# FFN 1's second matmul with seven tile pairs, four of them partly made ahead, in a streaming-encoder layer

## The chip, the cores and the metric

The kernel runs on one core of a Trainium2 chip, in one launch. The metric is the device time of a run in microseconds (us). The engines have short names in the profile: PE (TensorE, the matmuls), PEld (its weight loads, beside the matmuls), DVE (VectorE), ACT (ScalarE), POOL (GpSimd) and SP (SyncE, which here issues transfers only). SBUF is the memory on the chip beside the engines, PSUM holds the sums of matmuls in 8 banks of 128 x 512 fp32, and weights come from DRAM by transfers (DMA).

## The reference

One encoder layer on 512 tokens of width 1024, all in fp32. Two feed-forward layers (FFN) of inner width 2816 stand around a mixer of a recurrent branch and a windowed attention:

```python
def rms_norm(x, g):
    y = x * lax.rsqrt(jnp.mean(x * x, axis=-1, keepdims=True) + 1e-6)
    return y * g

def swiglu(x, w1, w3, w2):
    return (jax.nn.silu(x @ w1) * (x @ w3)) @ w2

f = swiglu(rms_norm(h, pre_g1), w1, w3, w2)          # FFN 1
h = h + 0.5 * rms_norm(f, post_g1)
u = rms_norm(h, mix_pre_g)
...                                                   # mixer: projections of u, scan, attention, gates
h = h + rms_norm(merged @ w_o, mix_post_g)
f = swiglu(rms_norm(h, pre_g2), w1, w3, w2)          # FFN 2
h = h + 0.5 * rms_norm(f, post_g2)
```

## The kernel before

**Precision.** Every operand of a matmul is split into a high part (a ScalarE copy to the float32r type) and a low part (a VectorE subtraction), and each product is three matmuls: high by high, high by low, low by high. `split2`, `split_to` and `task` with `flush` do the splits.

**The first matmuls of an FFN.** w1 and w3 have 22 column tiles each, named w1a, w3a for FFN 1 and w1b, w3b for FFN 2. FFN 1 computes the first `NC1` = 6 tiles of each in the plain way. The other 16 go in twos through `Pairs.run`: a job takes two neighbouring tiles of w1 or of w3 as a 2 x 2 matrix of blocks (a11, a12 are the halves of the first tile, a21, a22 of the second) and computes with seven block products instead of eight. There are 16 jobs, w1 and w3 in turn, numbered from 0; FFN 2 has 20. For a job VectorE forms four weight sums (`prep(m, 0)`): s12 = [a21 + a22 | that - a11] and s34 = [a11 - a21 | a12 - that]; steps 1 to 4 of `prep` split the tiles and the sums. In `run`, three PSUM banks bu, bx, bc take the products; ScalarE copies partial results to the tile ct (q1, q5, u), and VectorE adds them to later products: the result c = [c11 | c12; c21 | c22] of 256-token blocks. w1's result goes through SiLU, w3's is multiplied into it. The eighth block step of a job, `last`, runs inside the next job. A job prepares steps 1 to 4 of the next job and step 0 of the one after, and asks for the raw tiles of the job after that (`raws(n + 3)`). So a job has seven products of 12 matmuls of 256 columns; the first job has six.

**The order of work.** `point()` is called after each product of a job (and after each 12 matmuls of a plain unit, a half unit). `later(n, fn, rank)` puts work at the n-th point from now, lower rank first. The engines run their own queues in this order and wait for each other through the tiles only, so SyncE may issue a load as soon as the SBUF slot for it is free, long before the others come to the same place. There are `NSLOT` = 43 slots of 4 KB a partition; raw tiles, split tiles, sums and hidden tiles all use them.

**The second matmul.** `w2_gemm` multiplies the 22 hidden tiles by w2. `W2[name]` gives (W2_A, sizes, RF, fill): W2_A plain tiles first, then groups of tile pairs, the last RF tiles in `tok_finish` with the norms. A pair again takes seven products in place of eight; its weights are b11 and b21 (`w_b1`, one split of the first raw tile), t1 and t2 (`w_t12`), b22, t3 and t4. The hidden parts come from `h_plain`, `h_sums`, `h_rest`. A list of costs and due times (`plan`) is packed backwards from the due times, at 95% of VectorE's time, to find the point at which each part is made. For w2a (FFN 1) it is (6, (5,), 6, 0.95): six plain tiles, one group of five pairs, six tiles at the end. For w2b (FFN 2) it is (2, (4, 4), 4, 0.95).

**Pairs made ahead.** For the pairs in `PRE` the parts t1, t2, b22, t3 and t4 are made earlier (`pre_pair`), stored to DRAM by SyncE and loaded again in w2 (`w_load`). `PRE_AT` says in which stage, from which point and in which steps. One pair of w2a is made in the jobs of FFN 1; four pairs of w2b in the mixer's stages xr, xg and wg, five in all.

**Norms.** `post_norm` and `norms` sum squares on ScalarE, take a root (`root`), and `factor` forms a reciprocal on VectorE and one refinement step: r, e, r2. `softplus` is a chain of small VectorE steps on 8 columns, spread over the jobs.

## Time and profile before

| | |
|---|---|
| median of 3 runs | 1118.52 us (1118.45 to 1119.05) |
| the profiled execution's own time | 1118.27 us |
| its span, first to last instruction | 1116.5 us |
| granted TensorE clock, mean | 0.999 |
| busy: PE, PEld, DVE, ACT, POOL | 1107.2, 988.6, 920.1, 617.2, 34.7 us |
| transfers | 166.91 MB, mean 149 GB/s |

The pair jobs of FFN 1 run from about 78 to 234 us of the span, w2a from there to about 360, the mixer's projections from 364 on, FFN 2's jobs and w2b at the end.

A row of the groups has the line, engine and operation, out<-in by the program's names, the shapes, the count, then the busy time in us and the mean ns of one, and then the engine's idle time before these instructions with what ended it. A row of the timeline has start and duration in us. SPq and POOLq are the queues from which transfers are issued. The chain that ended last is followed back from the last instruction, at each step to what released it. Matmuls are pipelined: a PE row's duration is longer than the step from one matmul to the next.

### The profile page before, as it was taken

The page shows a single profiled execution, that of the slowest core. Times are in us where ns is not written, and L with a number is a line of the kernel's source. Part 1 is how long each engine was busy: PE and PEld are TensorE (multiplying, and loading weights), DVE is VectorE, ACT ScalarE, POOL GpSimd, SP SyncE. Part 2 cuts the span into 40 slices and gives each one's busy share as a digit, 9 for nine tenths or more (in the row PEclk, how much of TensorE's full clock was granted, in tenths as well). Part 3 has the DMA queues.
Part 4 walks back from the last instruction along what each step waited for, and adds up shares of the span by engine and source line. Part 5 has one row for each costly group of instructions (what it writes and reads, how often), then busy time and mean ns, then how long its engine had stood idle before and what let it go on. Part 6 is the DMA issues. An engine that isn't in the chain of part 4 may idle for free.

```text
span 1116.5 us, 17407 instructions
## 1 busy us (share of the span) xinstructions
PE 1107.2 (99%) x6679; PEld 988.6 (89%) x6679; DVE 920.1 (82%) x1622; ACT 617.2 (55%) x1088; POOL 34.7 (3%) x60
## 2 busy tenths in 40 slices
PE   9999999999999999999999999999999999999997
PEld 7889999988889887888888888888999999998886
DVE  5998889987987878897799876877788888887995
ACT  7455555574465468945656564456554555555352
POOL 0000000000000000001021111000000000000000
PEclk9999999999999999999999999999999999999999
DMA  9863334371565465445232235352423323257543
GB/s 353 138 163 104 114 114 131 125 274 38 170 226 182 159 226 189 153 149 200 103 95 76 84 106 196 127 186 104 161 83 107 114 85 105 95 191 283 177 179 114
DMA packets 52452, 166.91 MB, mean 149 GB/s; under 512 B 5712, under 2 KB 7248, under 8 KB 52368
## 3 DMA queue, kind: packets, MB, share of 16 engines
q1 hardware_dynamic: 49632, 156.97, 40.7%
q0 software_dynamic: 2448, 8.43, 4.0%
q8 instruction: 52, 0.85, 0.3%
q10 hardware_dynamic: 288, 0.39, 0.1%
q14 instruction: 32, 0.26, 0.1%
HBM read 139.57 MB, written 25.16 MB: 148 GB/s over the span
## 4 chain that ended last, share of the span: by engine, by line
PE 94%; ACT 3%; DVE 2%; issue 1%; DMA 0%; DVEq 0%; SPq 0%; ACTq 0%
PE c L899 11%; PE c L901 11%; PE c L900 11%; PE f L205 10%; PE f L206 10%; PE f L207 10%; PE acc L223 4%; PE acc L225 4%; PE acc L224 4%; PE acc L774 4%; PE acc L773 4%; PE acc L775 4%; PE pt L1508 1%; ACT ig_e L1308 1%; PE s L1472 1%; PE s L1471 1%
## 5 line engine op out<-in xcount | busy, mean ns | idle before, releaser
L205 PE MATMUL f<-uT,whi 128*128 128x512 f32 (+1 forms) x504 | 184.3, 366 | 0.0
L207 PE MATMUL f<-uT,whi 128*128 128x512 f32 (+1 forms) x504 | 182.7, 362 | 0.0
L206 PE MATMUL f<-uT,wlo 128*128 128x512 f32 (+1 forms) x504 | 182.7, 362 | 0.0
L899 PE MATMUL c<-Xh,whi 128*128 128x256 f32 x432 | 122.4, 283 | 0.1
L899 PE MATMUL c<-uT,whi 128*128 128x256 f32 x432 | 122.4, 283 | 0.0
L901 PE MATMUL c<-Xl,whi 128*128 128x256 f32 x432 | 122.3, 283 | 0.0
L900 PE MATMUL c<-Xh,wlo 128*128 128x256 f32 x432 | 122.3, 283 | 0.0
L901 PE MATMUL c<-uT,whi 128*128 128x256 f32 x432 | 122.3, 283 | 0.0
L900 PE MATMUL c<-uT,wlo 128*128 128x256 f32 x432 | 122.3, 283 | 0.0
L205 PEld LDWEIGHTS f<-uT,whi 128*128 128x128 f32 x504 | 95.1, 189 | 15.7 <-issue 1.3
L207 PEld LDWEIGHTS f<-uT,whi 128*128 128x128 f32 x504 | 95.1, 189 | 15.0
L206 PEld LDWEIGHTS f<-uT,wlo 128*128 128x128 f32 x504 | 95.2, 189 | 14.2
L196 DVE TENSOR_TENSOR wlo<-S,whi 128x1024 fp32r<-128x1024 f32 x72 | 87.8, 1219 | 14.2 <-ACT whi L195 14.2
L899 PEld LDWEIGHTS c<-Xh,whi 128*128 128x128 f32 x432 | 83.0, 192 | 0.3 <-ACT ct L978 0.3
L900 PEld LDWEIGHTS c<-Xh,wlo 128*128 128x128 f32 x432 | 83.0, 192 | 0.0
L899 PEld LDWEIGHTS c<-uT,whi 128*128 128x128 f32 x432 | 83.0, 192 | 0.0
L901 PEld LDWEIGHTS c<-Xl,whi 128*128 128x128 f32 x432 | 83.0, 192 | 0.0
L900 PEld LDWEIGHTS c<-uT,wlo 128*128 128x128 f32 x432 | 83.0, 192 | 0.0
L901 PEld LDWEIGHTS c<-uT,whi 128*128 128x128 f32 x432 | 83.0, 192 | 0.0
L195 ACT ACTIVATE whi<-S 128x1024 fp32r<-128x1024 f32 x72 | 72.6, 1050 | 0.0
L223 PE MATMUL acc<-whi,hT 128*128 128x512 f32 x144 | 56.2, 390 | 0.0
L224 PE MATMUL acc<-wlo,hT 128*128 128x512 f32 x144 | 56.1, 389 | 0.0
(411 smaller groups left out, 2781.7 us busy)
## 6 DMA issues: line engine op xcount, KB each, us to landing
raw_w1b<-in_w1b_dram SPq DMA_DIRECT2D x22, 512.0 KB, 4.2
raw_w3b<-in_w3b_dram SPq DMA_DIRECT2D x22, 512.0 KB, 4.3
raw_w3a<-in_w3a_dram SPq DMA_DIRECT2D x21, 512.0 KB, 4.5
raw_w2a<-in_w2a_dram SPq DMA_DIRECT2D x21, 512.0 KB, 5.7
raw_w1a<-in_w1a_dram SPq DMA_DIRECT2D x20, 512.0 KB, 4.9
raw_w2b<-in_w2b_dram SPq DMA_DIRECT2D x17, 512.0 KB, 4.3
h<-h SPq DMA_DIRECT2D x16, 512.0 KB, 3.4
raw_wg<-in_wg_dram SPq DMA_DIRECT2D x16, 512.0 KB, 4.2
```

The source lines that it names most:

```text
L195: act.activation(hi, src, AF.Copy)
L196: dve.tensor_tensor(out=lo, in0=src, in1=f32(hi), op=ALU.subtract)
L205: pe.matmul(ps[:, c0:c1], wh[:, s], h_, start=k == 0, stop=False)
L206: pe.matmul(ps[:, c0:c1], wl[:, s], h_, start=False, stop=False)
L207: pe.matmul(ps[:, c0:c1], wh[:, s], l_, start=False, stop=k == KT - 1)
L223: pe.matmul(acc[n], x[:, 0, c], wh[:, s], start=first, stop=False, skip_group_check=True)
L224: pe.matmul(acc[n], x[:, 0, c], wl[:, s], start=False, stop=False, skip_group_check=True)
L225: pe.matmul(acc[n], x[:, 1, c], wh[:, s], start=False, stop=last, skip_group_check=True)
L773: pe.matmul(b, h[:, c], wh, start=start and n_ == 0, stop=False, skip_group_check=True)
L899: pe.matmul(ps, wh[:, s], xh, start=first, stop=False, skip_group_check=True)
L900: pe.matmul(ps, wl[:, s], xh, start=False, stop=False, skip_group_check=True)
L901: pe.matmul(ps, wh[:, s], xl, start=False, stop=k == 3, skip_group_check=True)
```

## The change

FFN 1's w2 takes two plain tiles, groups of three and four pairs, and six tiles at the end. Four pairs (2, 4, 6, 8) are partly made ahead in the pair jobs, and for the same four the split of the first raw tile is made in the last jobs (`early_b1`). From job 3 on, FFN 1's jobs form two of the four weight sums in other ways: a21 is loaded from DRAM a second time into the sum's tile, and GpSimd issues a transfer that adds a22 from DRAM to it; a scaled ScalarE copy writes -a21, and another such transfer adds a11. In the jobs of both FFNs from the fourth on, the copy of the first product goes to the bank bc, and the product a12 is added to it there, so that VectorE's add falls away; SiLU and product then read the bank. `root` uses the reciprocal root in place of root and reciprocal. The tail of the last job (the first two hidden and weight tiles of w2) is divided over two places. The steps of softplus stand three points apart, and the w2b pairs in the stage xr take one step a point.

```diff
     def root(ss, v0):
-        act.activation(s, ss[:, 1:2], AF.Sqrt, scale=1.0 / D, bias=v0)
+        act.activation(s, ss[:, 1:2], AF.Abs_reciprocal_sqrt, scale=1.0 / D, bias=v0)
     def factor(ss, v0, s):
-        dve.reciprocal(r, s)
-        dve.scalar_tensor_tensor(out=e, in0=r, scalar=v, in1=r, op0=ALU.mult, op1=ALU.mult)
-        dve.scalar_tensor_tensor(out=r2, in0=e, scalar=-3.0, in1=r, op0=ALU.add, op1=ALU.mult)
+        dve.scalar_tensor_tensor(out=e, in0=s, scalar=v, in1=s, op0=ALU.mult, op1=ALU.mult)
+        dve.scalar_tensor_tensor(out=r2, in0=e, scalar=-3.0, in1=s, op0=ALU.add, op1=ALU.mult)
...
+    def early_b1(nm, f, at_):
+        k = order.index((nm, f))
+        def split():
+            hi, lo = slot([P, D], F32R, name="bh"), slot([P, D], F32R, name="bl")
+            split2(hi, lo, raws.pop(k))
+            EARLY_B1[nm, f] = hi, lo
+        later(at_ - 9, lambda: dma_one(k), 4)
+        later(at_, split, 4)
...
         def w_b1(f):
+            if (nm, f) in EARLY_B1:
+                hi, lo = EARLY_B1.pop((nm, f))
+                W[f] = {"b11": (hi[:, :QH], lo[:, :QH]), "b21": (hi[:, QH:], lo[:, QH:])}
+                return []
...
+        def plus(self, o, m, j, c):
+            pool.dma_start(out=o, in_=self.block(m, j, c), accum_op=ALU.add)
+        def sum1(self, m):
+            if self.add_from <= m < len(self.jobs):
+                self.s[m] = slot([P, 2 * QH], name="S12"), slot([P, 2 * QH], name="S34")
+                o = self.s[m][0][:, :QH]
+                sp.dma_start(out=o, in_=self.block(m, 1, 0))
+                self.plus(o, m, 1, 1)
+        def sums_ahead(self, m):
+            self.sum1(m)
+            later(SUM3, lambda: self.sum3(m), 2)
+        def sum3(self, m):
+            if self.add_from <= m < len(self.jobs):
+                o = (self.s.get(m) or self.w[m]["s"])[1][:, :QH]
+                r = raws[self.k0 + 2 * m + 1] if m in self.s else self.w[m]["r"][1]
+                act.activation(o, r[:, :QH], AF.Copy, scale=-1.0)
+                self.plus(o, m, 0, 0)
...
             if i == 0:
-                dve.tensor_tensor(out=s12[:, :QH], in0=a21, in1=a22, op=ALU.add)
+                if not self.made:
+                    dve.tensor_tensor(out=s12[:, :QH], in0=a21, in1=a22, op=ALU.add)
...
-                dve.tensor_tensor(out=s34[:, :QH], in0=a11, in1=a21, op=ALU.subtract)
+                if not self.made:
+                    dve.tensor_tensor(out=s34[:, :QH], in0=a11, in1=a21, op=ALU.subtract)
...
+                seed = n >= 3
+                h0 = 256 if seed else 0
...
                 mm_s(W["a11"], X["b11"], bu)
-                act.activation(q1, bu, AF.Copy)
+                act.activation(bc if seed else q1, bu, AF.Copy)
                 if n == len(self.jobs) - 1:
-                    tail()
+                    tail(1)
...
                 at(3)
+                if n == len(self.jobs) - 1:
+                    tail(2)
...
                 def c11():
-                    mm_s(W["a12"], X["b21"], bc)
+                    mm_s(W["a12"], X["b21"], bc, seed)
-                    dve.tensor_tensor(out=c[:, 0, :256], in0=bc, in1=q1, op=ALU.add)
+                    if not seed:
+                        dve.tensor_tensor(out=c[:, 0, :256], in0=bc, in1=q1, op=ALU.add)
+                    elif first:
+                        act.activation(c[:, 0, :256], bc, AF.Silu)
+                    else:
+                        c1 = self.c1[f]
+                        dve.tensor_tensor(out=c1[:, 0, :256], in0=bc, in1=c1[:, 0, :256], op=ALU.mult)
...
-                    act.activation(c[:, 0, :], c[:, 0, :], AF.Silu)
+                    act.activation(c[:, 0, h0:], c[:, 0, h0:], AF.Silu)
...
-                    dve.tensor_tensor(out=c1[:, 0, :], in0=c1[:, 0, :], in1=c[:, 0, :], op=ALU.mult)
+                    dve.tensor_tensor(out=c1[:, 0, h0:], in0=c1[:, 0, h0:], in1=c[:, 0, h0:], op=ALU.mult)
...
                 self.raws(n + 3)
+                self.sums_ahead(n + 3)
...
-    pairs_a = Pairs("w1a", "w3a", NC1, X1, hid)
+    pairs_a = Pairs("w1a", "w3a", NC1, X1, hid, ADD_FROM)
...
-            later(at1 + i, step, 4)
+            later(at1 + i * SP_STEP, step, 4)
...
+ADD_FROM = 3
+SUM3 = 6
-W2 = {"w2a": (6, (5,), 6, 0.95), "w2b": (2, (4, 4), 4, 0.95)}
+W2 = {"w2a": (2, (3, 4), 6, 0.95), "w2b": (2, (4, 4), 4, 0.95)}
-PRE = {"w2a": (6,), "w2b": (2, 4, 6, 8, 14)}
+PRE = {"w2a": (2, 4, 6, 8), "w2b": (2, 4, 6, 8, 14)}
-PRE_AT = {"w1a": [("w2a", 6, 63, PRE_JOB)], "xr": [("w2b", 2, 1, 2), ("w2b", 8, 6, 2), ("w2b", 14, 11, 2)], ...}
+PRE_AT = {"w1a": [("w2a", 2, 0, (0, 1, 2, 9, 10, 14, 15, 16, 17, 18, 22, 23, 29, 30, 31)), ("w2a", 4, 28, (...)), ("w2a", 6, 49, (...)), ("w2a", 8, 77, (...))], "xr": [("w2b", 2, 1, 1), ("w2b", 8, 6, 1), ("w2b", 14, 12, 1)], ...}
+EARLY = {"w1a": [("w2a", 2, 79), ("w2a", 4, 86), ("w2a", 6, 100), ("w2a", 8, 108)]}
+SP_STEP = 3
```

More of the change, by code (lines that the diff above doesn't have):

```diff
@@ L263, in root @@
         s = small(1, "s")
-        act.activation(s, ss[:, 1:2], AF.Sqrt, scale=1.0 / D, bias=v0)
+        act.activation(s, ss[:, 1:2], AF.Abs_reciprocal_sqrt, scale=1.0 / D, bias=v0)
         return s
     def factor(ss, v0, s):
-        v, r, e, r2 = (small(1, x) for x in ("v", "r", "e", "r2"))
+        v, e, r2 = (small(1, x) for x in ("v", "e", "r2"))
         dve.scalar_tensor_tensor(out=v, in0=ss[:, 1:2], scalar=1.0 / D, in1=v0, op0=ALU.mult, op1=ALU.add)
-        dve.reciprocal(r, s)
-        dve.scalar_tensor_tensor(out=e, in0=r, scalar=v, in1=r, op0=ALU.mult, op1=ALU.mult)
-        dve.scalar_tensor_tensor(out=r2, in0=e, scalar=-3.0, in1=r, op0=ALU.add, op1=ALU.mult)
+        dve.scalar_tensor_tensor(out=e, in0=s, scalar=v, in1=s, op0=ALU.mult, op1=ALU.mult)
+        dve.scalar_tensor_tensor(out=r2, in0=e, scalar=-3.0, in1=s, op0=ALU.add, op1=ALU.mult)
         return r2
@@ L535, in pre_pair @@
             later(at0 + (i * step if isinstance(step, int) else step[i]), lambda fns=fns: [fn() for fn in fns], 4)
+    EARLY_B1 = {}
+    def early_b1(nm, f, at_):
[6 more added lines that the diff above has]
+        later(at_, split, 4)
     def pre_at(where):
+        for nm, f, at_ in EARLY.get(where, ()):
+            early_b1(nm, f, at_)
         for i, at_ in FIRST_AT.get(where, ()):
@@ L685, in w2_gemm @@
                 d = 0.68 * i
-                plan += [(ta + d, 1.1, h_plain, f), (ta + d, 1.22, w_b1, f)]
+                plan += [(ta + d, 1.1, h_plain, f), (ta + d, 0 if (nm, f) in EARLY_B1 else 1.22, w_b1, f)]
                 plan += [(ta + 2 * PB + d, 2.1, h_sums, f), (ta + 4 * PB + d, 0.7, h_rest, f)]
@@ L904, in hybrid_layer, with __init__ @@
     class Pairs:
-        def __init__(self, na, nb, f0, X, hid):
+        def __init__(self, na, nb, f0, X, hid, add_from=99):
+            self.add_from = add_from
             self.jobs = [(nm, f) for f in range(f0, FT, 2) for nm in (na, nb)]
@@ L911, in __init__, with block @@
             self.k0 = order.index((na, f0))
-            self.w, self.c1 = {}, {}
+            self.w, self.c1, self.s = {}, {}, {}
+        def block(self, m, j, c):
+            nm, f = self.jobs[m]
+            return a[nm][(f + j) * P : (f + j + 1) * P, c * QH : c * QH + QH]
+        def plus(self, o, m, j, c):
[15 more added lines that the diff above has]
+                self.plus(o, m, 0, 0)
         def raws(self, m):
@@ L928, in prep @@
                     self.raws(m)
-                s12, s34 = slot([P, 2 * QH], name="S12"), slot([P, 2 * QH], name="S34")
+                self.made = m in self.s
+                s12, s34 = self.s.pop(m, None) or (slot([P, 2 * QH], name="S12"), slot([P, 2 * QH], name="S34"))
                 self.w[m] = {"r": (raws.pop(k), raws.pop(k + 1)), "s": (s12, s34)}
@@ L1244, in hybrid_layer, with w2_ahead @@
     }
-    def w2_ahead():
-        hid.to(1)
-        split_to(st["split"] + 1)
-        hid.to(2)
+    def w2_ahead(n):
+        hid.to(n)
         split_to(st["split"] + 1)
     pre_at("w1a")
-    softplus(6, 9)
+    softplus(*SP_AT)
     pairs_a.run(w2_ahead, late)
```

3 lines of the change are left out of this document (2 added, 1 removed).

## The prediction

> **What bounds the kernel now.** I read the page's busy times first, then the shares of the chain that ended last, then that chain in order of time, the windows by stage, the groups by line, and last the transfer queue's own rows.
>
> ```profile
> span 1116.5 us, 17407 instructions
> PE 1107.2 (99%) x6679; PEld 988.6 (89%) x6679; DVE 920.1 (82%) x1622; ACT 617.2 (55%) x1088; POOL 34.7 (3%) x60
> PE 94%; ACT 3%; DVE 2%; issue 1%; DMA 0%; DVEq 0%; SPq 0%; ACTq 0%
> ```
>
> TensorE is busy for 99% of the span and makes 94% of the chain. So a change pays in two ways only: fewer matmuls, or less waiting in the few places where TensorE waits. What the other engines gain or lose counts only where it makes TensorE late. The windows (columns: stretch and its length, then busy time and instruction count of PE, PEld, DVE, ACT, POOL, the granted clock, the DMA share, GB/s) show the stages:
>
> ```profile
> 85.00:235.00 150.00, 149.94 (x1245) 149.52 (x1245) 132.76 (x221) 83.51 (x138) 0.00 (x0) 1.00 0.39 128
> 235.00:315.00 80.00, 80.00 (x355) 66.24 (x354) 72.52 (x112) 41.16 (x64) 1.10 (x2) 1.00 0.46 160
> 395.00:405.00 10.00, 10.00 (x45) 8.29 (x45) 6.45 (x10) 4.76 (x5) 0.00 (x0) 1.00 0.80 275
> 445.00:455.00 10.00, 9.51 (x46) 6.89 (x45) 8.86 (x14) 9.82 (x15) 0.00 (x0) 1.00 0.31 105
> 455.00:465.00 10.00, 9.22 (x64) 8.47 (x63) 7.34 (x11) 9.76 (x14) 0.00 (x0) 1.00 0.67 211
> ```
>
> The pair jobs of FFN 1 (85 to 235) and its w2 (from 235) keep TensorE full; VectorE is the engine with the least room there: 132.76 of 150 us, then 72.52 of 80 us. TensorE is idle for 0.49 + 0.78 = 1.27 us between 445 and 465, in the mixer's first projections.
>
> **Fewer matmuls in w2.** In the chain, matmuls of 512 columns follow one another like this (17 steps lie between the two rows):
>
> ```profile
> 1105.98 0.23 PE acc L223
> ...
> 1109.83 0.24 PE acc L225
> ```
>
> 3.85 us / 17 = 0.2265 us each. The durations of 390 ns in the groups overlap, so the step is the price. A plain tile of w2 issues 4 token tiles x 2 halves x 3 = 24 such matmuls, two of them 48; a pair issues 7 products x 2 x 3 = 42. The change turns four plain tiles into two pairs: 96 - 84 = 12 matmuls fewer, **-2.72 us**. All of it lies on the path, as TensorE has no idle time from 235 to 315.
>
> **VectorE in the pair jobs.** The prices:
>
> ```profile
> L196 DVE TENSOR_TENSOR wlo<-S,whi 128x1024 fp32r<-128x1024 f32 x72 | 87.8, 1219 | 14.2 <-ACT whi L195 14.2
> L996 DVE TENSOR_TENSOR cc<-c,ct 128x256 f32<-128x256 f32 x36 | 15.0, 417 | 2.0 <-PE c L901 2.0
> L1013 DVE TENSOR_TENSOR cc<-cc,cc 128x512 f32<-128x512 f32 x18 | 12.3, 683 | 0.1
> L949 DVE TENSOR_TENSOR S<-raw_w3a,raw_w3a 128x512 f32<-128x512 f32 x8 | 5.5, 684 | 0.0
> L978 ACT ACTIVATE ct<-c 128x256 f32<-128x256 f32 x36 | 13.7, 381 | 50.4 <-PE c L901 49.9
> ```
>
> Removed: two weight sums (2 x 0.68) in each of the 13 jobs from job 3 on, 17.8 us. The seeded block sum removes one 256-column add (0.42) in the six w1 jobs among them, 2.5 us; in the seven w3 jobs the add becomes the product itself and the 512-column product shrinks to 256, 0.68 + 0.42 - 0.84 = 0.26 each, 1.8 us. Together 22.1 us. Added: three more pairs made ahead, each five 512-column subtractions, one 1024-column and three 512-column low parts, 5 x 0.68 + 1.22 + 3 x 0.68 = 6.7 us, so 20.0; and four early first-column splits at 1.22, 4.9. Together 24.9. Net +2.8 us, while VectorE has 150 - 132.76 = 17.2 us free there. ScalarE takes the negated copy (one 512-column instruction), the high parts and the split SiLU; it had 66 us free. The copied product has the size of the L978 copy that it replaces (0.38); its target bank is in PSUM, which this trace shows for no copy. It is needed three products later than it is made, 3 x 12 matmuls of about 0.12 us (1245 in 150 us), so 4.3 us, and its price, between 0 and twice 0.38, is covered by that. The softplus steps go from one a product to one in three: same work, thinner. I cost all this at **0**; without the free VectorE time it would be 2.8 us.
>
> **The adding transfers.** A weight sum now goes: SyncE loads one 256 KB block behind the two raw tiles of the same job, GpSimd waits for it and adds the other block in place, VectorE builds the next sum on it. No row shows an adding transfer; the nearest are plain ones:
>
> ```profile
> xt<-in_xT_dram SPq DMA_DIRECT2D x7, 256.0 KB, 4.2
> BT<-bias_scr POOLq DMA_DIRECT2D x16, 128.0 KB, 3.4
> bc_ffn_post_g<-in_ffn_post_g_dram POOLq DMA_DIRECT2D x2, 512.0 KB, 6.2
> bc_mix_pre_g<-in_mix_pre_g_dram POOLq DMA_DIRECT2D x1, 512.0 KB, 8.5
> 305.91 0.56 POOL L248 DMA_DIRECT2D bc_ffn_post_g<-in_ffn_post_g_dram  x1 [270.31 <-DVE acc L732]
> 101.69 1.31 SPq L142 DMA_DIRECT2D raw_w1a<-in_w1a_dram  x2
> ```
>
> Two raw issues 1.31, block 4.2, GpSimd's issue 0.56, landing between 3.4 (half the bytes) and 8.5 (twice the bytes): 9.5 to 14.6 us after the raw issue. I take 6.2 for the landing, on the dear side because the transfer also reads what it adds to: 12.3 us. The cover is how far SyncE runs ahead:
>
> ```profile
> 92.97 0.80 SPq L142 DMA_DIRECT2D raw_w3a<-in_w3a_dram  x2
> 114.05 0.68 DVE L946 TENSOR_TENSOR S<-raw_w3a 128x512 f32<-128x512 f32 x1
> 189.38 0.80 SPq L142 DMA_DIRECT2D raw_w1a<-in_w1a_dram  x2
> 204.55 0.68 DVE L946 TENSOR_TENSOR S<-raw_w1a 128x512 f32<-128x512 f32 x1
> 199.57 1.59 SPq L142 DMA_DIRECT2D raw_w3a<-in_w3a_dram  x2
> 215.60 0.69 DVE L946 TENSOR_TENSOR S<-raw_w3a 128x512 f32<-128x512 f32 x1
> ```
>
> Raw tiles are issued 21.1 us before their first sum, and 15.2 us once a pair's stores stand in SyncE's queue. Counted back from the last job, 15, whose two rows close the fence (lead 16.0), the others belong to jobs 5 and 14. All leads exceed 12.3, so I cost the wait at 0. The second sum (negated copy, then an add) is read a job later by a split, about 9 us after the copy, against 0.6 + 0.56 + 6.2. Behind a late sum stand the rest of VectorE's queue and, from there, the splits of the next job.
>
> ```profile
> 305.00:315.00 10.00, 10.00 (x46) 8.29 (x45) 9.82 (x13) 7.71 (x11) 1.10 (x2) 1.00 0.84 285
> ```
>
> The Trainium skill, "SBUF — State Buffer" (section on the shared port pair), speaks against this: GpSimd writes the descriptors of its transfers through ports shared with VectorE, and a VectorE instruction in a two-port mode, or with two SBUF inputs against a GpSimd instruction that reads SBUF, shuts it out; a transfer of 620 ns is said to become 3100 ns. By that each adding transfer would cost up to 2.5 us more, an estimate from that page. Here GpSimd's issue at 305.91 took 0.56 us in a stretch where VectorE was 98% busy, so the rows do not show it.
>
> **VectorE in w2, and the second group.** Out of the 72.52 us go the splits of four plain tiles (4 x 1.9 = 7.6), two first-column splits (2.4) and one pair's t12 to t4 (6.7). In come the hidden parts of two more pairs, 2 x (1024 + 256 + 4 x 256 + 512 columns, 4.1) and a second group's twelve 512-column adds (8.2): 72.2 us. The time falls from 80 to 77.3, the free part from 7.5 to 5.1. A second group brings a boundary. FFN 2's w2 has one already, with two plain tiles ahead. Of TensorE's waits in the whole span, the first of these rows is its longest there; the others belong to the next part:
>
> ```profile
> PEld acc L774 <- DVE bl L559: 0.4, 1, 0.4
> PE v L1407 <- DVE wlo L161: 0.8, 1, 0.8
> PE r L1304 <- DVE xcs L1295: 0.5, 1, 0.5
> ```
>
> I take **+0.4 us**, between 0 and 2.4 (all of the free time that is lost turns into a wait). The four premade pairs also bring 3 x 2.5 MB of stores and as much of reloads; at a DMA share of 0.39 and 0.46 there is room, and the reloads are issued 8 to 14 us ahead.
>
> **The mixer's first projections.** The other two waits above, 0.8 and 0.5, make up the 1.27 us idle. The work for FFN 2's w2 pairs runs in the same stretch, one step in two half units (2.72 us each, 12 x 0.2265); the change makes it one step a half unit. The first begins here in the chain:
>
> ```profile
> 374.12 0.23 PE f L206
> ```
>
> Half unit n ends at 374.1 + 2.72 n. Of pair 8, three subtractions and two low parts (3.4 us) come from half units 16 to 20 to 11 to 13, ahead of about 410, and pair 14 ends at 20 instead of 27. These go out of the way of the stall:
>
> ```profile
> 440.55 0.68 DVE L459 TENSOR_TENSOR rawp<-rawp 128x512 f32<-128x512 f32 x1
> ...
> 453.42 0.68 DVE L488 TENSOR_TENSOR pb<-rawp,pb 128x512 fp32r<-128x512 f32 x1
> ```
>
> VectorE has 3.55 us free from 395 to 405 to take them. ScalarE stays at 98%, so the whole wait need not go. Bounds: -1.27 (all idle time) and +0.5 (the new place delays a product as much as L1304 waits now); I take **-0.9 us**.
>
> **The root.** One reciprocal fewer in each of 20 norms. Only the last is on the path:
>
> ```profile
> 1110.81 0.69 DVE fg L284
> 1111.50 0.07 DVE v L270
> 1111.57 0.09 DVE r L271
> 1111.65 0.02 issue
> 1111.68 0.23 DVE e L272
> L264 ACT ACT_TABLE_LOAD x3 | 3.8, 1283 | 0.8 <-DVE v L258 0.8
> ```
>
> Without it, e follows v: **-0.1 us**. The table is loaded three times for 20 roots, once a finishing stage, and I keep that count for the new function.
>
> **The sum.** 1118.27 (the profiled execution: span 1116.5 and 1.77 around it) - 2.72 + 0.4 - 0.9 - 0.1 = 1114.95. The median of the runs lies 0.25 above that execution, so 1115.2.
>
> **Rivals.**
> A: the sums come late, slower. The mechanism: premade parts are stored by SyncE in order, each store waiting for a low part, and the early splits hold up to eight more slots, so SyncE stops running ahead and raw tiles go out only at the end of the job before. The lead is then one job, 10.1 us (jobs 5 to 14: 90.5 / 9), against 12.3: 2.2 us late, less some 0.9 of free VectorE time a job ((17.2 - 2.8) / 16), 1.3 us. In seven jobs (2, 4, 6, 8, 9, 11, 12) such a store stands at most four products ahead of the raw tiles: 7 x 1.3 = 9.1, 1124.3. It decides once the lead is under 11.4 us. For it: the lead has already shrunk from 21.1 to 15.2 with one premade pair. Against: it is still 3 us more than needed, and splits are made a job ahead. Chance 0.15.
> B: VectorE in w2 is late by all of the lost free time, +2.4 instead of +0.4: 1117.2. For it: w2 starts its groups 10.9 us after the last job instead of 32.6, with no slack to catch up. Against: the first group's parts are all made. Chance 0.11.
> C: the moved steps of FFN 2's pairs delay the products, +0.5 instead of -0.9: 1116.6. Chance 0.07.
> D: the root does not do what it says: if the new function shares no table with the squares, each root brings two loads. At the end one of them (1.28 and the root's 0.29 against the 0.69 of L284) adds 0.9, and each of the two other finishing stages may show one: 0.9 + 2.6, 1118.7. Against: the three loads for 20 roots now. Chance 0.05.
>
> **How the numbers follow.** The forecast has 0.62. Its own range is 1114.3 (no boundary wait, all of the 1.27) to 1116.3. A measurement of this kernel can tell about 0.2% from no change, so faster means under 1116.3 and slower over 1120.8. Faster: the forecast and half of C, 0.65. Same: B, D and the rest of C, 0.20, of which 0.02 goes to slower, since each of them can meet a milder form of A: 0.18. Slower: A and that, 0.17. The range 1113.9 to 1120.0 takes in B, C and D and leaves out A and what may lie below.
>
> **What would show it.** Matmuls at L223 with hT: 112 instead of 144; those of the pair products 28 more a line. From 235 on, w2's end 2.3 to 2.7 us earlier relative to the jobs' end; no VectorE wait on a GpSimd transfer at the sums; GpSimd issues near 0.56 us; idle time of TensorE between 445 and 465 under 0.5 us; three loads at the root's line. I am wrong if the pair jobs last longer than now, if TensorE waits more than 1 us in w2, or if the stall before 465 stays.

## The result, and the profile after

The changed kernel takes 1124.88 us (median; 1123.58 to 1125.22) against 1118.49 us (1118.06 to 1119.05) for the kernel before beside it: 1.0055 of its time, 95% interval 1.0042 to 1.0067. It is slower by 6.4 us where 3.3 us less was forecast. The profiled execution took 1123.58 us, the shortest of its four runs.

```profile
span 1121.8 us, 17658 instructions
PE 1108.1 (99%) x6667; PEld 988.1 (88%) x6667; DVE 914.1 (81%) x1602; ACT 631.4 (56%) x1129; POOL 57.3 (5%) x86
PE 81%; DVE 8%; DMA 4%; ACT 3%; issue 2%; SPq 0%; DVEq 0%; POOLq 0%; ACTq 0%
```

These are the three lines of the page shown for before. The 12 matmuls are gone (6679 to 6667), and yet PE's busy time is not lower: some matmuls ran at half the clock (below), and a row's duration, longer than the step, covers short gaps. What changed is the chain: VectorE's share rose from 2% to 8%, and transfers, which had none, have 4%.

Stage lengths, read from the first and the last matmul of each stage in the timeline:

| stage | before | after | difference | forecast |
|---|---|---|---|---|
| pair jobs of FFN 1 | 161.55 | 169.38 | **+7.83** | 0 |
| w2 of FFN 1, to its last group | 96.36 | 94.54 | -1.82 | -2.72 + 0.4 |
| mixer's projections | 110.57 | 109.75 | -0.82 | -0.9 |
| FFN 2's jobs | 201.48 | 201.48 | 0 | 0 |
| after the last matmul | 6.83 | 6.94 | +0.11 | -0.1 |

The rows between the stages (the start, +0.21, and the six tiles at the end of w2, -0.25) cancel; the sum is the +5.3 us by which the span grew. So all of the loss lies in the pair jobs. The gains in w2 and in the mixer came within 0.5 us of their forecasts; the root's 0.1 did not come. The windows of these stages (columns as before):

```profile
85.00:235.00 150.00, 145.77 (x1189) 144.36 (x1188) 127.12 (x209) 94.50 (x161) 21.73 (x25) 0.99 0.86 261
235.00:315.00 80.00, 79.75 (x376) 66.70 (x375) 69.89 (x121) 41.03 (x71) 1.09 (x2) 1.00 0.62 221
445.00:455.00 10.00, 10.00 (x46) 8.01 (x47) 8.03 (x13) 9.79 (x15) 0.00 (x0) 1.00 0.91 311
455.00:465.00 10.00, 10.00 (x52) 8.12 (x49) 6.27 (x10) 9.80 (x15) 0.00 (x0) 1.00 0.17 52
```

In the jobs TensorE issued 1189 matmuls in 150 us instead of 1245. VectorE did not become busier: 127.12 us instead of 132.76, fewer jobs' work in the same time. A slower stage in which the tight engine is *less* busy points to a new wait. The transfers' share rose from 0.39 to 0.86. In the mixer (the last two rows) TensorE's idle 1.27 us is gone.

VectorE's waits from 72 to 245 us (the line that waited <- what it waited for: us in total, times, longest). First before, then after:

```profile
DVE w L196 <- ACT w L195: 8.7, 8, 1.7
DVE wlo L196 <- ACT whi L195: 6.3, 12, 1.0
```

```profile
DVE w L196 <- ACT w L195: 9.1, 9, 1.7
DVE S L993 <- DMA S<-in_w3a_dram: 8.1, 4, 2.8
DVE S L993 <- DMA S<-in_w1a_dram: 4.3, 1, 4.3
DVE wlo L196 <- ACT whi L195: 1.7, 4, 0.9
```

L993 reads the first sum, a21 + a22, to build the next one. Five times it stood waiting for the adding transfer, 8.1 + 4.3 = 12.4 us. The chain shows the links of one such wait, the base loaded by SyncE, then the adding transfer, then the VectorE instruction (start, duration, what):

```profile
142.15 7.05 DMA S<-in_w3a_dram
149.77 6.95 DMA S<-in_w3a_dram
156.74 0.70 DVE S L993
```

From the base's issue to the sum 14.6 us passed. The transfers of the jobs in groups (count, KB, median us from issue to landing) and the queues' shares of the engines' time from 85 to 235 us:

```profile
q1 hardware_dynamic: 11043, 32.40, 59.4%
q0 software_dynamic: 3600, 6.56, 25.9%
...
raw_w3a<-in_w3a_dram SPq DMA_DIRECT2D x12, 512.0 KB, 6.7
...
S<-in_w3a_dram POOLq DMA_DIRECT2D x13, 256.0 KB, 6.6
S<-in_w1a_dram POOLq DMA_DIRECT2D x12, 256.0 KB, 6.4
...
S<-in_w1a_dram SPq DMA_DIRECT2D x6, 256.0 KB, 6.8
S<-in_w3a_dram SPq DMA_DIRECT2D x6, 256.0 KB, 7.6
```

The adding transfer itself takes about what was forecast (6.2 taken, medians of 6.4 to 6.6 measured). Its base does not: 6.8 to 7.6 us against the 4.2 taken.

The TensorE side of it, PE's waits in the whole span:

```profile
PE c L918 <- DVE wlo L196: 1.9, 1, 1.9
...
PE c L917 <- ACT ct L1038: 1.5, 1, 1.5
```

These are VectorE's lateness come through, directly and by way of ScalarE: before the copy of the second row empties its PSUM bank, ScalarE stands 3.9 us (to 227.07) waiting for a sum of a premade pair, which VectorE makes behind a late first sum. The first wait had a sequel (start, duration):

```profile
193.38 0.28 PE L917 MATMUL c<-Xh,whi 128*128 128x256 f32 x1
195.61 0.39 PE L918 MATMUL c<-Xh,wlo 128*128 128x256 f32 x1 [1.95 <-DVE wlo L196]
...
196.97 0.42 PE L918 MATMUL c<-Xh,wlo 128*128 128x256 f32 x1
197.18 0.41 PE L919 MATMUL c<-Xl,whi 128*128 128x256 f32 x1
```

```profile
198.00:200.00 2.00, 2.00 (x12) 2.00 (x11) 2.00 (x5) 0.00 (x1) 0.00 (x0) 0.51 1.01 369
```

After 2.2 us from one start to the next the steps of 256 columns went from 0.12 to 0.21 us and the granted clock to 0.51, for 16 matmuls from 196.55 on, 3.4 us, of which about 1.5 us are lost. TensorE's six pauses in the jobs (2.2, 1.7, 0.7, 0.6, 0.5 and 0.3 us from one start to the next) cost 5.4 us over the usual step of 0.12 us, and the step behind each is 0.1 us longer; with the slow clock that is 7.5 of the 7.8 us.

### The profile page after: what moved, and what is told of

Read it like the earlier page. It is cut to its first block, busy times and chain, and to the rows that moved or that the text cites. A ratio compares the mean times of both kernels' runs of the same rounds, so it can differ in the third digit from the quotient of the medians.

```text
span 1121.8 us, 17658 instructions
## 1 busy us (share of the span) xinstructions
PE 1108.1 (99%) x6667; PEld 988.1 (88%) x6667; DVE 914.1 (81%) x1602; ACT 631.4 (56%) x1129; POOL 57.3 (5%) x86
## 4 chain that ended last, share of the span: by engine, by line
PE 81%; DVE 8%; DMA 4%; ACT 3%; issue 2%; SPq 0%; DVEq 0%; POOLq 0%; ACTq 0%
PE f L205 10%; PE f L207 10%; PE f L206 10%; PE c L917 8%; PE c L919 8%; PE c L918 8%; PE acc L224 3%; PE acc L792 3%; PE acc L225 3%; PE acc L791 3%; PE acc L223 3%; PE acc L793 3%; DMA S<-in_w3a_dram 2%; DMA S<-in_w1a_dram 1%; PE pt L1564 1%
## 5 line engine op out<-in xcount | busy, mean ns | idle before, releaser
L206 PEld LDWEIGHTS f<-uT,wlo 128*128 128x128 f32 x504 | 95.2, 189 | 14.4
L196 DVE TENSOR_TENSOR wlo<-S,whi 128x1024 fp32r<-128x1024 f32 x72 | 87.8, 1219 | 14.4 <-ACT whi L195 14.4
L195 ACT ACTIVATE whi<-S 128x1024 fp32r<-128x1024 f32 x72 | 74.4, 1051 | 1.8 <-DVE S L993 1.7
L1541 ACT ACTIVATE P<-P,ng 128x256 f32<-128x256 f32 (+1 forms) x64 | 30.1, 471 | 25.8 <-DVE ng L1536 18.7
L224 PE MATMUL acc<-wlo,hT 128*128 128x512 f32 x112 | 43.7, 391 | 0.4 <-DVE wlo L573 0.4
```

The source lines that it names most:

```text
L195: act.activation(hi, src, AF.Copy)
L196: dve.tensor_tensor(out=lo, in0=src, in1=f32(hi), op=ALU.subtract)
L206: pe.matmul(ps[:, c0:c1], wl[:, s], h_, start=False, stop=False)
L224: pe.matmul(acc[n], x[:, 0, c], wl[:, s], start=False, stop=False, skip_group_check=True)
```

## The experiments

**My theory:** from the issue of the job's raw tiles the first sum's chain takes 14.1 to 16.5 us in the five jobs that waited (5, 7, 9, 12 and 15), while VectorE came for the sum after 11.7 to 14.2 us. So VectorE waits, and VectorE has not the room in the jobs that I gave it. **Rivals:** (P) the extra work on VectorE alone does it; (Q) the load on the transfer engines delays the raw tiles, whichever sums are made by it; (R) SyncE's queue, with the raw tiles and the stores in it, is what sends the base late. All kernels below compute the whole reference. "Jobs" is the stage length as in the table above, read from the profiled execution. In the expectations my theory is called L, and the rivals P and Q are V and B.

**e1: the first sum asked for a job earlier**, nothing else moved.

```diff
         def sums_ahead(self, m):
-            self.sum1(m)
+            if m == self.add_from:
+                self.sum1(m)
+            self.sum1(m + 1)
```

> The changed kernel, with the first adding sum of each job asked for one job earlier (both transfers of it; two more slots held). Theory L (the first sum comes late: base load plus adding transfer took 14 to 16 us, and SyncE, stopped by the stores of premade parts, starts them less than that ahead): VectorE's waits on S at the sums (12.4 us in 5 waits) fall under 2 us, the pair jobs shrink from 169.4 us to 161.5 to 163, the time is 1115.5 to 1118. Rival V (VectorE has too much work in the jobs, the wait only shows where it runs dry): the jobs stay above 166 us, over 1121. Rival B (bandwidth: 261 GB/s at a share of 0.86, every transfer is late): the same bytes, so the waits turn up at the raw tiles instead, over 1121.

Measured: 1118.06 us (1116.5 to 1119.62), ratio 0.9996 [0.9987, 1.0006]; jobs 162.70.

```profile
85.00:235.00 150.00, 149.51 (x1240) 148.73 (x1239) 133.41 (x218) 98.88 (x169) 20.70 (x24) 1.00 0.91 273
```

VectorE waits for no sum any more, and 6.7 of the 7.8 us are back, with the same transfers at an even higher share (0.91). So the load by itself (Q) isn't the cause, and P is worth at most the 1.15 us that remain. It is the lateness of the first sum. The median lies at the upper edge of my range, 1.2 us above the profiled execution (1116.87), and the ten runs spread over 3.1 us; what spreads them is not shown.

**e2, e3, e4: one kind of sum, or none, by transfers.** e2 makes only the second sum (negated copy, then added a11) by transfer, e3 only the first, e4 neither; VectorE makes the others.

e2:

```diff
-                sp.dma_start(out=o, in_=self.block(m, 1, 0))
-                self.plus(o, m, 1, 1)
-                if not self.made:
-                    dve.tensor_tensor(out=s12[:, :QH], in0=a21, in1=a22, op=ALU.add)
+                dve.tensor_tensor(out=s12[:, :QH], in0=a21, in1=a22, op=ALU.add)
```

e3:

```diff
-                if not self.made:
-                    dve.tensor_tensor(out=s34[:, :QH], in0=a11, in1=a21, op=ALU.subtract)
+                dve.tensor_tensor(out=s34[:, :QH], in0=a11, in1=a21, op=ALU.subtract)
...
-                act.activation(o, r[:, :QH], AF.Copy, scale=-1.0)
-                self.plus(o, m, 0, 0)
+                pass
```

e4:

```diff
-ADD_FROM = 3
+ADD_FROM = 99
```

> The changed kernel, with the first sum (a21 + a22) back on VectorE and only the second sum made by an adding transfer. Theory L: no wait for a first sum is left; VectorE gets 13 x 0.68 = 8.9 us more, 127.1 + 8.9 = 136 of 150 us, still under the 132.8 + 4 at which the kernel before ran without stalls or nearly so; jobs 161.5 to 164 us, time 1115.5 to 1119. Rival V: VectorE's load decides, jobs longer than 169.4, over 1125. Rival B: 6.5 MB of 39 MB fewer, the stall falls by a part, 1120 to 1123.

> The changed kernel, with the second sum back on VectorE and only the first made by an adding transfer. Theory L: the late sum stays and VectorE has 8.9 us more to catch up with: 1124 to 1129. Rival V: 1126 to 1131 by the load alone. Rival B: 3.3 MB fewer bytes, 1122 to 1124. Beside the run with the second sum alone, this tells which of the two sums costs.

> The changed kernel with no adding transfers, all four sums on VectorE. Theory L: no such wait; VectorE has 127.1 + 17.8 = 144.9 of 150 us, so it is close to the bound itself: 1117 to 1122. Rival V: VectorE decides, 12 to 18 us longer than the changed kernel, over 1135. Rival B: 9.8 MB fewer, share near 0.6, 1117 to 1120.

Measured: e2 1119.0 us, 1.0004 [0.9995, 1.0014], jobs 164.49. e3 1123.08 us, 1.0037 [1.0025, 1.0049], jobs 168.19. e4 1126.53 us, 1.0072 [1.0055, 1.0088], jobs 171.76. The windows of the jobs for e2 and e4, and e3's waits for sums:

```profile
85.00:235.00 150.00, 148.83 (x1229) 147.61 (x1228) 139.74 (x227) 98.18 (x167) 11.25 (x13) 1.00 0.71 228
```

```profile
85.00:235.00 150.00, 143.63 (x1171) 141.00 (x1169) 141.50 (x233) 84.43 (x144) 0.00 (x0) 1.00 0.53 192
```

```profile
DVE S L990 <- DMA S<-in_w1a_dram: 3.3, 1, 3.3
DVE S L990 <- DMA S<-in_w3a_dram: 2.2, 2, 1.6
```

e2 and e3 give VectorE the same work, 13 x 0.68 = 8.9 us more than the change does; the first sum's transfer costs 3.7 us more than the second's, and waits 5.5 us. Of the three, my theory's range held for e2 alone, at its edge: e3 came out under it (1124 to 1129) and inside B's, and e4 outside all of them. So the theory had the place, and B is out by e1, but neither gave the sizes. And e4 tells what my forecast missed on the other side: without any transfer for sums VectorE lacks room by 10 us, although its 17.8 + 2.8 us of added work exceed the 17.2 us free by only 3.4. It was busy for just 141.50 of 150 us there: some of the free time can't be used. P is thus real, but for e4, not for the change.

**e5: the sums alone, in the kernel before.** Its code for both sums is put into the kernel before; no pairs made ahead beyond its one.

```diff
+ADD_FROM = 3
+SUM3 = 6
...
                 self.raws(n + 3)
+                self.sums_ahead(n + 3)
```

> The kernel before with nothing changed but the two adding sums of jobs 3 to 15 (six plain tiles and one group in w2, one premade pair, no seeded block sum). Theory L: the sums come late only because the stores of three more premade pairs stop SyncE and their bytes slow every transfer; with one premade pair the chain (two raw issues, base, GpSimd's issue, adding transfer) is near 12 us against a lead of 15 to 21 us, no VectorE wait on S over 1 us in all, 1117.9 to 1118.8. Rival C (an adding transfer is too slow by itself, whatever stands around it): waits on S as in the changed kernel, 1121 to 1125.

Measured: 1118.67 us, 1.0 [0.9991, 1.0009], jobs 161.51, no wait for a sum above 0.2 us.

```profile
85.00:235.00 150.00, 149.94 (x1245) 149.56 (x1244) 117.22 (x195) 90.61 (x152) 21.76 (x25) 1.00 0.71 195
```

The adding transfers harm nothing by themselves, though their chain is no shorter here: from the issue of the raw tiles it took 10.9 to 17.8 us, in the changed kernel 11.1 to 17.7, and not the 12 expected. What differs is the lead: VectorE came for the sum 15.4 to 24.0 us after that issue, in the changed kernel 11.7 to 22.8. The two halves of the change only fail together, since the pairs made ahead shorten the lead of a chain that was already longer than forecast. VectorE fell to 117.22 us here, and nothing was gained, because TensorE is full.

**e6: GpSimd issues the base too**, so that it does not stand behind SyncE's raw tiles.

```diff
-                sp.dma_start(out=o, in_=self.block(m, 1, 0))
+                pool.dma_start(out=o, in_=self.block(m, 1, 0))
```

> The changed kernel, with the base of the first sum (a21) loaded through GpSimd's queue in place of SyncE's. If the order in SyncE's queue (behind stores and raw tiles) makes the sum late, the base now starts as soon as its slot is free and GpSimd has issued the job's earlier transfers: waits on S under 6 us (12.4 before), 1117.5 to 1121. If the bandwidth does (each transfer takes near 7 us however it is issued), the waits stay near 12 us and the time at 1123 to 1126.

Measured: 1123.87 us, 1.0041 [1.0027, 1.0055], jobs 169.43. No gain:

```profile
DVE S L993 <- DMA S<-in_w3a_dram: 8.2, 4, 3.5
DVE S L993 <- DMA S<-in_w1a_dram: 3.0, 1, 3.0
```

In GpSimd's queue the bases of jobs 5, 7, 9, 12 and 15 went out only 0.2 to 2.3 us earlier than in SyncE's, and those of jobs 6, 8, 10 and 13, which stand there behind adding transfers that wait for bases, 3.8 to 6.7 us later; jobs 6 and 13 now waited too. One wait was put in place of another, so this tells of R only that a second queue is no way out.

**e7: only the mixer's finer steps, in the kernel before** (three of w2b's five premade pairs).

```diff
-PRE_AT = {... "xr": [("w2b", 2, 1, 2), ("w2b", 8, 6, 2), ("w2b", 14, 11, 2)], ...}
+PRE_AT = {... "xr": [("w2b", 2, 1, 1), ("w2b", 8, 6, 1), ("w2b", 14, 12, 1)], ...}
```

> The kernel before with nothing changed but the steps of FFN 2's premade pairs in the stage xr (one step a half unit; pair 14 from 12). Both theories: the stretch from the last w2a transposes to the v product gets 0.6 to 1.0 us shorter, as between before and the changed kernel (110.57 against 109.75 us): 1117.4 to 1117.9. If the shorter stretch was owed to something earlier in the changed kernel, it stays 1118.4.

Measured: 1117.89 us (1117.39 to 1118.63), 0.9994 [0.9984, 1.0003]. The time can't tell 0.8 us; the stretch can: 110.57 before, 109.75 here and in the changed kernel alike, and TensorE is full from 445 to 465:

```profile
445.00:455.00 10.00, 10.00 (x50) 7.77 (x49) 7.09 (x11) 9.81 (x15) 0.00 (x0) 1.00 0.46 149
455.00:465.00 10.00, 10.00 (x72) 9.38 (x71) 7.34 (x11) 9.80 (x15) 0.00 (x0) 1.00 0.21 54
```

**e8: what blocks VectorE's free time.** In the eight w1 jobs ScalarE makes both SiLU before the high part of a22, which VectorE waits for (L196 <- L195, 8.7 us before, 9.1 after). If that is the part of the free time that can't be used, then e2 with the split ahead of the SiLU must lose its 2.9 us. On e2:

```diff
                 if first:
+                    self.prep(n + 1, 4)
                     act.activation(c[:, 0, h0:], c[:, 0, h0:], AF.Silu)
                     act.activation(c[:, 1, 256:], c[:, 1, 256:], AF.Silu)
...
-                self.prep(n + 1, 4)
+                if not first:
+                    self.prep(n + 1, 4)
```

> The run with the second sum alone (first sum back on VectorE), and in w1's jobs ScalarE makes the high part of a22 ahead of the two SiLU instead of behind them. VectorE waited 8 times, 8.7 us in all, for that high part in every kernel here. If the rest of the jobs' loss is VectorE's load (137 us of work and 9 us of such waits in 150), the jobs go from 164.5 us to 161.6 to 163, and the time to 1116 to 1117.8, below both kernels. If the stalls left are of another kind, it stays at 1118.5 to 1119.5.

Measured: **1116.30 us** (1115.91 to 1116.93), 0.998 [0.9971, 0.9988]; jobs 162.04.

```profile
85.00:235.00 150.00, 149.61 (x1244) 149.16 (x1243) 140.53 (x230) 99.54 (x171) 11.27 (x13) 1.00 0.73 234
```

The row of L196 <- L195 for a22 has gone from the waits (that for the other high parts rose, from 0.9 us in e2 to 5.6), and TensorE is nearly full with VectorE at 140.53 us, a load at which e4 lost 10 us. This version beats both kernels.

**e12: the same swap in the kernel before.**

```diff
                 if first:
+                    self.prep(n + 1, 4)
                     act.activation(c[:, 0, :], c[:, 0, :], AF.Silu)
```

> The kernel before with nothing changed but the order of the high part of a22 and the SiLU. TensorE is not waiting in its pair jobs, so both theories say no change, 1118.2 to 1118.8, although 8.7 us of VectorE's waits go in FFN 1 alone.

Measured: 1118.21 us, 0.9999 [0.999, 1.0008], jobs 161.47 (161.55 before). The waits for a22 are gone here too, but those for the other high parts rose from 6.3 us to 13.7: with nothing more to do, VectorE waits elsewhere. Nothing is gained; room is worth something only where work wants it.

**e10, e11: combinations.** e10 is e8 with the parts made in w2 of FFN 1 packed 4.5 us ahead of their due times in place of 2.5; e11 is e1 with the swap. On e8:

```diff
-            cur = min(cur, due_ - W2_LEAD) - cost / W2_FILL
+            cur = min(cur, due_ - (4.5 if nm == "w2a" else W2_LEAD)) - cost / W2_FILL
```

> The run e8 with the list of w2a packed 4.5 us ahead of the due times in place of 2.5. The wait of 0.6 us that every kernel with seven pairs shows where the last plain tiles begin is VectorE's: if it comes from the packing, w2a's stretch (94.5 us) gets 0.5 to 0.8 us shorter, 1115.4 to 1116.0; if VectorE has no free time before it, nothing changes, 1116.1 to 1116.6.

> Both adding sums, the first asked for a job earlier (as in e1), and the high part of a22 ahead of the SiLU (as in e8). If e1's spread (1116.5 to 1119.6) is owed to the adding transfers at a share of 0.91, the spread stays and the median lies at 1116.5 to 1118; if it was VectorE's lack of room, the run is as steady as e8 and faster: 1115 to 1116.

Measured: e10 1117.72 us, 0.9993 [0.9984, 1.0002]: w2 took 95.43 instead of e8's 94.51, the wait moved to its start, one gap of 1.78 us at 245.1. That is slower than both of its expectations. e11 1117.91 us (1117.4 to 1119.27), 0.9998 [0.9989, 1.0007], jobs 163.17, the branch in which the spread stays. VectorE's waits are now for high parts:

```profile
DVE wlo L196 <- ACT whi L195: 12.5, 12, 2.5
```

The longest of them, at 128.30, is for a raw tile's high part and not a sum's, and e12, without any adding transfer, has 13.7 us of the same row; so these do not explain e11. Ahead of its pause of 0.9 us at 201.5 ScalarE stood 2.7 us waiting for a slot that the store of a premade part held. That the two slots more which the longer lead holds are the reason is not shown.

With the lead the change comes no further than the kernel before; only the version with one adding transfer a job, that of the second sum, is faster than both.

**e9: the pairs' stores on ScalarE's queue**, two products later, so that SyncE never stops at one (rival R, my rival A's mechanism).

```diff
         def store(i, name):
             x = t.pop(name)
+            if nm == "w2a":
+                later(2, lambda: send(i, x), 5)
+                return
...
+        def send(i, x):
+            if i == 0:
+                for d, y in zip(dram[:2], x):
+                    act.dma_start(out=d, in_=f32(y))
```

> The changed kernel, with the stores of FFN 1's premade parts issued from ScalarE's queue, two points later, in place of SyncE's. If SyncE's stops at those stores are what starts the first sum late, SyncE now runs ahead as far as the slots allow: waits on S fall under 3 us in all (12.4 in the changed kernel), the jobs from 169.4 us to 161.6 to 164, the time to 1116.5 to 1119. If the slots hold SyncE back just as much, or the bandwidth decides, the waits stay over 8 us and the time over 1121.

Measured: 1124.35 us, 1.0054 [1.0041, 1.0068], jobs 169.74. No gain, in another way:

```profile
SPq L142 <- PE c L929: 68.6, 12, 10.1
DVE wlo L196 <- DMA pre_w2a<-pl: 4.3, 1, 4.3
DVE S L1003 <- DMA S<-in_w3a_dram: 2.9, 1, 2.9
DVE S L1003 <- DMA S<-in_w1a_dram: 2.2, 1, 2.2
```

At jobs 5, 7 and 11 VectorE now came 16.7, 16.5 and 16.2 us after the base's issue, where in the changed kernel it came after 11.7, 12.3 and 13.2 us, and the waits for the first sum fell from 12.4 to 5.1 us. So the stores did hold SyncE, as its own waits between 85 and 235 us say (the longest row before, then after):

```profile
SPq L142 <- PE c L901: 35.1, 6, 10.2
```

```profile
SPq L495 <- DVE pb L487: 41.4, 9, 11.6
```

L142 asks for raw tiles and waits for slots, L493 and L495 (before, L494 and L496) are the stores and wait for VectorE's and ScalarE's parts. Before, SyncE waits 107 us in all at L142 and 22 at the stores; after, 21 and 89; in e9, 117 at L142. So SyncE runs ahead again as far as the slots allow. But the late issue of job 14 stayed (194.88 against 194.94 us); the chain of jobs 9 to 12 grew to 17.6 to 20.3 us, with bases that took 7.5 to 10.1, and the waits are now at jobs 10 and 11; and the parts keep their slots longer, for which VectorE waits 4.3 us (the second row) and ScalarE 6.1. How much each of these costs is not shown.

**e13: no early first-column splits.** They hold up to eight slots.

```diff
-EARLY = {"w1a": [("w2a", 2, 79), ("w2a", 4, 86), ("w2a", 6, 100), ("w2a", 8, 108)]}
+EARLY = {}
```

> The changed kernel without the four early splits of first raw tiles (they are made in w2, as the kernel before does); up to eight slots come free late in the pair jobs, and the jobs lose 4.9 us of VectorE's work, which w2 gets. If held slots set the time at which SyncE can issue, the raw tiles of the last jobs go out earlier (194.9 and 209.1 us in the changed kernel) and the stalls after 200 us (0.4, 1.6 us) go: the jobs 166 to 167.5 us in place of 169.4; w2 loses 1 to 3 us of it again. If the slots are not it, the issue times stay within 1 us and the jobs at 169.

Measured: 1125.55 us, 1.0065 [1.0049, 1.0082]; jobs 163.77, w2 100.60. Raw tiles went out 2 to 3 us earlier (192.92 and 206.03 instead of 194.94 and 209.07), the waits for the first sum fell to 9.7 us, and the jobs lost 5.6 of their 7.8 us. But VectorE came earlier by as much: its lead from the raw tiles was 16.1 and 11.8 us at the last two jobs, against 17.1 and 11.7. So this doesn't show that the slots shorten the lead; the 4.9 us of VectorE's work that left the jobs fit the gain. And w2 paid 6.1 us: 4.65 us without a matmul at 247.0, then 3.4 us at half clock. The early splits are not free in the jobs, and not to be left out either.

**e14: e8 without the seeded block sum.** On e8:

```diff
-                seed = n >= 3
+                seed = n >= 99
```

> The run e8 without the seeded block sum in either FFN: VectorE adds the copy as in the kernel before. 4.3 us of VectorE's work come back in FFN 1's jobs, where e8 has 140.5 of 150 us busy. If VectorE's room decides there, the jobs get 1 to 4 us longer, 1117.3 to 1120; if the copy into PSUM has a price of its own that this saves, it is as fast as e8 or faster, 1115.8 to 1116.3. FFN 2's jobs, where nothing waits, stay at 201.5 us by both.

Measured: 1117.37 us (1116.88 to 1118.32), 0.9991 [0.9982, 1.0]; jobs 162.85 instead of 162.04, FFN 2's jobs 201.48 in both. The seeded sum is worth 0.8 us where VectorE is tight, and 0 in FFN 2's jobs, where it isn't.

## Why the prediction was wrong

**The step that failed: "All leads exceed 12.3, so I cost the wait at 0."** It measured 12.4 us of VectorE waits, in five of thirteen jobs, and both sides of the comparison were off.

The lead, from the issue of the raw tiles to VectorE's coming for the sum, I read in the kernel before (15.2 to 21.1 us) and left there. With the change's own stores in SyncE's queue it was 11.7 to 14.2 us in the jobs that waited. The prediction had said itself that a premade pair had taken the lead from 21.1 to 15.2; three more could not be costed at the same lead.

The chain took 14.1 to 16.5 us in these jobs and not 12.3. The mis-sized term is the base, 4.2 forecast and 5.8 to 8.1 measured; the two raw issues before it took 1.0 to 2.0 us instead of 1.31. From the base's landing to GpSimd's issue passed 0.53 to 0.56 us, as forecast. The adding transfer, which I had to guess, took 4.0 to 7.9 us, 6.6 in the mean against 6.2; between bounds of 3.4 and 8.5 that is in part luck. Why the base takes longer than the seven loads that priced it is not settled. Their stretch (the first 10 us) has a share of 0.65, then of 1.00, so the share alone can't be it; but each follows a load of 128 KB at most, where the base follows two raw tiles of 512 KB, which take 6.6 to 6.7 us themselves.

The two sides don't weigh the same: in e5 the chain is as long, and the lead of the kernel before still covers it.

**The second step that failed: "I cost all this at 0"**, with 17.2 us of free VectorE time as cover. That time was not free: 8.7 us of it were the eight waits for the high part of a22, at a place where ScalarE is always late, and they did not shrink when VectorE had more to do (9.1 us after). If the rest can be used, that is 17.2 - 8.7 = 8.5 us, less the change's net work 2.8: 5.7. Against that stand 12.4 us of waits: 6.7 us too many, and 1.5 for the half clock make 8.2, where 7.8 were measured. The same count for the other runs (work and waits added to the change, room, excess, and the jobs' measured growth over 161.55):

| run | added work + waits | room | excess | measured |
|---|---|---|---|---|
| e4 | 17.8 | 5.7 | 12.1 | 10.2 |
| e9 | 5.1 + 4.3 | 5.7 | 3.7, with the half clock 5.2 | 8.2 |
| e6 | 11.2 | 5.7 | 5.5 | 7.9 |
| e3 | 8.9 + 5.5 | 5.7 | 8.7 | 6.6 |
| e2 | 8.9 | 5.7 | 3.2 | 2.9 |
| e8 (a22 ahead) | 8.9 | 14.4 | 0 | 0.5 |
| e14 (a22 ahead) | 8.9 + 4.3 | 14.4 | 0 | 1.3 |
| e1 | 0 | 5.7 | 0 | 1.15 |
| e13 (no early splits) | 9.7 | 10.6 | 0 | 2.2 |

The net work itself was near its forecast: over the jobs VectorE was busy for 142.82 us before (72 to 234) and 144.34 after (72 to 242). The count tells the runs that lose much from those that lose little, within some 3 us, but not their order: e3 counts more than the changed kernel, e6 and e9, and its jobs are shorter than all of theirs. It knows totals, not when a wait falls. That the order at a22 costs time where VectorE is loaded is shown by e2 against e8, one edit apart (2.4 us); that just the 8.7 us are the unusable part, and the count beyond that, is an argument.

**Rival A** had the outcome, the sums late, and most of the mechanism. SyncE did stop running ahead at the stores (its waits under e9), and in the seven jobs that it named the raw tiles went out at the end of the job: these are the tiles of jobs 5, 7, 9, 11, 12, 14 and 15, three ahead, and all five waits of 0.4 us and more fall on them. The lead there fell to 11.7 us at the least, where it had one job, 10.1. Its chain was too short (12.3 against 14.1 to 16.5), so that the lateness was 0.4 to 4.3 us, where it had 2.2. That its 1124.3 us lies so near the 1124.88 measured is in part luck: there were fewer waits, some of them longer, and 1.5 us at half clock that it didn't have. Of its two holds, e9 shows the stores; for the slots of the early splits e13 shows none. How far slots and transfer load limit the lead and the chain once the stores are out of the way stays open; more slots than 43 weren't tried.

**What held.** The 12 matmuls: L223 with hT has 112, and w2 is shorter by 1.82 = 2.72 - 0.90. The loss was mis-sized, 0.9 instead of 0.4, inside its bounds, and isn't at the boundary: no step is longer where the second group begins (281.5). About 0.7 of it lies a little behind the start of the last plain tiles (steps of 0.23 us, one of 0.80, the next 0.34), 0.15 at 308.5:

```profile
PE acc L224 <- DVE wlo L573: 0.4, 1, 0.4
```

So rival B had the right cause, VectorE late in w2, at a third of its price. The mixer's steps: -0.82 for -0.9, alone in e7; C is out. D is out: the table loads are three as before. But the root gave 0 and not -0.1. Before and after, from the start of fg to that of o, 1.32 us (1110.81 to 1112.13, and):

```profile
1116.01 0.69 DVE fg L283
1116.70 0.08 DVE v L270
1116.78 0.03 issue
1116.81 0.02 DVEq L271
1116.83 0.06 issue
1116.88 0.23 DVE e L271
...
1117.33 0.75 DVE o L293
```

The reciprocal's 0.09 us and the issue after it are gone, and the same time goes to issuing e; I read that as time which the reciprocal had hidden.

## What to carry to other kernels

Before an engine's free time is used as cover, take off the waits that more work would not shorten: a row of the waits that names a neighbour which is late by its own order is not room, and such an order may be a cheap thing to change (e8), but only where work wants the room (e12). Price a transfer by a row with like transfers ahead of it in its queue, and read the lead of a chain across queues as it will be with the change's own stores in it: the lead is the time at which the reader would come, without the wait. Where a chain comes late, ask for it a job earlier (e1) or send fewer links through it (e8); another queue for the same chain gave nothing (e6, e9).

## What the runs showed of the hardware

- **An adding transfer is dear in engine time.** In the jobs, 6.56 MB of them took 25.9% of the transfer engines' time and 32.40 MB of plain ones 59.4%: 3.9% against 1.8% a MB, over twice as much. Packets of the same size show it too: of 2 KB they took 192 ns in the mean with the add and 95 without. Their landing time (6.4 to 6.6 us for 256 KB) doesn't show it, since the plain base beside them takes as long.
- **The clock fell after a short pause.** 2.2 us between the starts of two matmuls (193.38 to 195.61) were followed, 0.9 us later, by 3.4 us at half the granted clock; 2.18 us in e9, 1.4 us later, and 4.65 us in e13, at their end, were too. 1.7 us, 1.8 us (e10), 1.9 us (e3 and e4) and, in e6, another 2.2 us were not. The Trainium skill, "TensorE: Matmul & The Clock Gate" (part 1), describes a free-running window of about 3.4 us, whose idleness halves the clock. The 3.4 us at half agree. The same 2.2 us with and without the drop would fit a window that runs freely, but no run here shows where it begins. And the pause was shorter than the gap of about 3.4 us that this part names as the limit.
- **GpSimd's issue of an adding transfer** took 0.86 us beside a VectorE that was busy for 85% of the time (127.12 of 150 us), against 0.54 to 0.56 for the plain ones of L248. The chain does not get longer by it, since the 6.4 to 6.6 us to landing count from the start of that issue. The 2.5 us more that the prediction drew from the Trainium skill, "SBUF — State Buffer", were not seen. That page measured them beside a copy on VectorE, while in the jobs VectorE's work is almost all sums, differences and products of two inputs.
